# A two-layer trunk: SwiGLU blocks by seven block products in place of eight

## The chip, the cores and the metric

The kernel runs on one core of a Trainium2 chip. The metric is the device time of one execution in microseconds (us), and a run's figure is the median of its executions. The core has a matrix engine (TensorE: PE in the profile, PEld for its weight loads), VectorE (DVE), ScalarE (ACT), GpSimd (POOL) and SyncE (SP), which issues the transfers. SBUF is the memory on the core, PSUM the small one that the matrix engine writes.

## What is computed

Two layers over 512 tokens of width 1024, all float32. Each layer has a SwiGLU block, a token mixer, and a second SwiGLU block; so there are four SwiGLU blocks with an inner dimension of 2816, and two mixers (a convolution beside sparse attention; a short convolution beside stick-breaking attention).

```python
def _swiglu(x, w_in, w_out):
    gate, up = jnp.split(x @ w_in, 2, axis=-1)
    return (jax.nn.silu(gate) * up) @ w_out
...
    for layer in range(DEPTH):
        x = x + 0.5 * _swiglu(_rmsnorm(x, ffn1_norm[layer]), ffn1_w_in[layer], ffn1_w_out[layer])
        h = _rmsnorm(x, mix_norm[layer])
...
        x = x + y
        x = x + 0.5 * _swiglu(_rmsnorm(x, ffn2_norm[layer]), ffn2_w_in[layer], ffn2_w_out[layer])
    return _rmsnorm(x, final_norm)
```

## The kernel before

The stream `xT` stays in SBUF, transposed: 8 tiles of 128 channels by 512 tokens. A float32 operand is used as two parts, a high one in the matrix engine's float32r type and the rest, so one product of a weight block takes three matmuls: high by high, high by low, low by high (`mm3`, lines 112 to 115). The two parts are made by `split` (lines 80 to 87): ScalarE writes the high part (line 83), VectorE subtracts it from the source (line 84); with a scale per partition these are lines 86 and 87. `load_w` (lines 98 to 110) loads a piece of a weight of up to 128x1024 (line 103, from SP's queue) and splits it; raw pieces and split pieces have three buffers each.

`ffn` (lines 178 to 220) is a SwiGLU block. For each of 22 pairs of a gate tile and an up tile it loads the two weight pieces and runs 8 x 3 matmuls of 128x512 for each, into a PSUM bank `gu`. VectorE multiplies both by `rstd`, the reciprocal norm by token (lines 191 and 195), ScalarE applies SiLU (193), VectorE multiplies (197), and the activation is split (199). Then `down` (lines 201 to 210) makes each of the 8 output tiles `fo` with 22 x 3 matmuls, and VectorE adds half of it to `xT` (line 210). In the last block of all, the last output tile is made in two halves of 256 tokens, so that the final norm of the first half (`last`, lines 795 to 822) runs beside the second half.

After each output tile, `nxt` (for the next norm: `Norm.add`, lines 139 to 141) makes the next operand of that tile, the tile times its gain, split (`operand`, 122 to 127), and adds its square to a running sum (`square`, 129 to 137: ScalarE squares, GpSimd adds in line 136, VectorE adds the last). `finish` turns the sum into `rstd` (`rsqrt_rows`, 146 to 175: eight small matmuls, twelve small VectorE instructions, a transpose). At the start the tiles of x and the first two weight pieces are loaded in turn, so that the first product runs while x comes in (lines 751 to 762).

The order on each queue is made by the framework's scheduler, which places instructions by their priority (the order in which they are traced) and by a simulated time line; a tile's slot is given out again when its last reader is placed. GpSimd does little beside the sums of squares: in `mixer0` it scales probabilities (line 622).

Of the kernel before, what the change touches and what calls it, by code (L numbers as in the profile page):

```python
# [7 lines left out]
F32 = mybir.dt.float32  # L8
# [6 lines left out]
P = 128  # L15
# [16 lines left out]
OFFT = [0, 512, 1024, 896]  # L32
# projections beside each head
FILL = [3, 1, 1, 2, 1, 1, 2, 1]
# [11 lines left out]
def trunk(ctx: ExitStack, tc: tile.TileContext, a: dict, out: bass.AP):  # L46
# [7 lines left out]
    xnp = ctx.enter_context(tc.tile_pool(name="xnp", bufs=16))  # L54
# [25 lines left out]
    def split(hi, lo, src, scale=None):  # L80
        """hi + lo = src (times a per-partition scale), both float32r."""
# [36 lines left out]
    class Norm:  # L118
        def __init__(self, col):
            self.col, self.h, self.l, self.ss = col, [], [], []  # L120

        def operand(self, k):
            hi = xnp.tile([P, T], F32R, tag="xn", name=nm("xh"))
            lo = xnp.tile([P, T], F32R, tag="xn", name=nm("xl"))
            split(hi, lo, xT[:, k, :], prm[:, self.col + k:self.col + k + 1])
            self.h.append(hi)
            self.l.append(lo)

        def square(self, k):
            sq = cp.tile([P, T], F32, tag="c", name=nm("sq"))  # L130
            S.activation(sq, xT[:, k, :], AF.Square)  # L131
            if k == 0:
                self.ss = [sq]
            else:
                s2 = cp.tile([P, T], F32, tag="c", name=nm("ss"))
                (V if k == KD - 1 else G).tensor_tensor(s2, self.ss[0], sq, ALU.add)  # L136
                self.ss = [s2]

# [39 lines left out]
    def ffn(norm, w_in, w_out, nxt, ph, halves=None):  # L178
        act = []
        tiles = [ph.rtile("act", "act", T) for _ in range(2 * NP)]  # L180
        for p_ in range(NP):
            ps = []
            for gu in range(2):
                hi, lo = load_w(w_in[p_, :, gu], KD * P)
# [742 lines left out]
```

## Time and profile before

| | |
|---|---|
| median of 3 runs (lowest, highest) | 1989.33 us (1986.51, 1997.28) |
| span of the profiled execution | 1989.2 us |
| PE busy | 1964.9 us |
| DVE, ACT, POOL busy | 1003.6, 713.8, 107.1 us |
| read from HBM | 175.74 MB, 89 GB/s over the span |

The profiled span is within 0.2 us of the median, so sums made against the span hold for the median as well. A matmul's duration in the profile overlaps with its neighbours; its cost in a stream is the step from one start to the next.

### The profile page before, as it was taken

Reading aid. Unit: us, or ns where it says so; the run is one execution under the profiler, and the core shown is the slowest. Engines: PE = TensorE matmul, PEld = TensorE weight load, DVE = VectorE, ACT = ScalarE, POOL = GpSimd, SP = SyncE. Lnnn points to the kernel's source line nnn. Section 1 sums busy time; section 2 is a strip of 40 time slices with the busy share of each in tenths; the row PEclk is TensorE's granted clock in tenths of the full one; section 3 lists DMA queues with packets and bytes.
Section 4 is the critical chain, followed back from the end, with each engine's and each line's share of the span. In section 5 each row is a group of like instructions: output and inputs, shape, how many; then the busy total and the mean of one; then the engine's idle time right before and its main releaser. Section 6 shows DMA issues by size and latency. Waiting matters only on the chain.

```text
span 1989.2 us, 22201 instructions
## 1 busy us (share of the span) xinstructions
PE 1964.9 (99%) x8886; PEld 1598.3 (80%) x8886; DVE 1003.6 (50%) x1488; ACT 713.8 (36%) x1052; POOL 107.1 (5%) x112
## 2 busy tenths in 40 slices
PE   8999999989999999999999999999999999999998
PEld 7888888778767888888888888888877888888887
DVE  6444432499976544443334444333668744444323
ACT  5332222236675323322223333222544433322222
POOL 2000001000322100000000000000000010000000
PEclk9999999999989999999999999999999999999999
DMA  5222333232101223233332222333311222223332
GB/s 180 96 96 96 96 93 97 87 108 75 43 1 34 98 97 100 96 93 91 95 102 97 96 95 96 89 97 101 96 64 53 85 96 96 96 95 96 96 93 96
DMA packets 52086, 179.27 MB, mean 90 GB/s; under 512 B 5776, under 2 KB 6160, under 8 KB 51984
## 3 DMA queue, kind: packets, MB, share of 16 engines
q1 hardware_dynamic: 51840, 177.73, 28.0%
q8 instruction: 69, 1.13, 0.2%
q14 instruction: 33, 0.27, 0.0%
q10 hardware_dynamic: 144, 0.14, 0.0%
HBM read 175.74 MB, written 2.10 MB: 89 GB/s over the span
## 4 chain that ended last, share of the span: by engine, by line
PE 97%; DVE 1%; ACT 0%; DMA 0%; issue 0%; DVEq 0%; SPq 0%
PE gu L113 16%; PE gu L115 16%; PE gu L114 16%; PE fo L115 8%; PE fo L114 8%; PE fo L113 8%; PE ac L115 3%; PE ac L114 3%; PE ac L113 3%; PE mo L114 1%; PE mo L115 1%; PE mo L113 1%; PE pt L286 1%; PE ss L613 1%; PE po L297 1%; PE po L296 1%
## 5 line engine op out<-in xcount | busy, mean ns | idle before, releaser
L83 ACT ACTIVATE whi<-raw 128x1024 fp32r<-128x1024 f32 (+3 forms) x339 | 350.4, 1034 | 1072.5 <-PE gu L114 572.5
L84 DVE TENSOR_TENSOR wlo<-raw,whi 128x1024 fp32r<-128x1024 f32 (+3 forms) x339 | 405.7, 1197 | 302.6 <-ACT whi L83 300.0
L113 PE MATMUL gu<-xh,whi 128*128 128x512 f32 x1408 | 548.5, 390 | 6.7 <-ACT whi L83 6.7
L114 PE MATMUL gu<-xl,whi 128*128 128x512 f32 x1408 | 548.9, 390 | 0.0
L115 PE MATMUL gu<-xh,wlo 128*128 128x512 f32 x1408 | 548.5, 390 | 0.0
L113 PEld LDWEIGHTS gu<-xh,whi 128*128 128x128 f32 x1408 | 265.0, 188 | 61.5 <-ACT whi L83 6.9
L115 PEld LDWEIGHTS gu<-xh,wlo 128*128 128x128 f32 x1408 | 264.9, 188 | 55.2
L114 PEld LDWEIGHTS gu<-xl,whi 128*128 128x128 f32 x1408 | 264.9, 188 | 55.0
L115 PE MATMUL fo<-act,wlo 128*128 128x512 f32 (+1 forms) x726 | 281.9, 388 | 0.0
L113 PE MATMUL fo<-act,whi 128*128 128x512 f32 (+1 forms) x726 | 281.8, 388 | 0.0
L114 PE MATMUL fo<-act,whi 128*128 128x512 f32 (+1 forms) x726 | 281.8, 388 | 0.0
L195 DVE TENSOR_TENSOR u<-gu,rstd 128x512 f32<-128x512 f32 x88 | 60.8, 691 | 263.0 <-PE gu L115 263.0
L114 PEld LDWEIGHTS fo<-act,whi 128*128 128x128 f32 x726 | 136.3, 188 | 31.2
L115 PEld LDWEIGHTS fo<-act,wlo 128*128 128x128 f32 x726 | 136.3, 188 | 31.1
L113 PEld LDWEIGHTS fo<-act,whi 128*128 128x128 f32 x726 | 136.3, 188 | 31.0
L191 DVE TENSOR_TENSOR g<-gu,rstd 128x512 f32<-128x512 f32 x88 | 60.8, 691 | 182.7 <-PE gu L115 172.4
L113 PE MATMUL ac<-xh,whi 128*128 128x512 f32 x288 | 112.9, 392 | 0.6 <-ACT whi L83 0.6
L114 PE MATMUL ac<-xl,whi 128*128 128x512 f32 x288 | 113.1, 393 | 0.0
L115 PE MATMUL ac<-xh,wlo 128*128 128x512 f32 x288 | 113.0, 393 | 0.0
L136 POOL TENSOR_TENSOR ss<-sq,sq 128x512 f32<-128x512 f32 x7 | 11.5, 1648 | 1331.8 <-ACT sq L131 1331.8
L83 ACT ACTIVATE act<-h 128x512 fp32r<-128x512 f32 x88 | 55.8, 634 | 58.3 <-DVE h L197 58.3
L136 POOL TENSOR_TENSOR ss<-ss,sq 128x512 f32<-128x512 f32 x35 | 56.5, 1616 | 307.9 <-ACT sq L131 245.6
(277 smaller groups left out, 1854.7 us busy)
## 6 DMA issues: line engine op xcount, KB each, us to landing
raw<-in_w_in SPq DMA_DIRECT2D x174, 512.0 KB, 3.7
raw<-in_w_out SPq DMA_DIRECT2D x66, 448.0 KB, 3.3
raw<-in_w_out SPq DMA_DIRECT2D x33, 512.0 KB, 3.5
raw<-in_cd_a SPq DMA_DIRECT2D x20, 512.0 KB, 3.5
raw<-in_ab_a SPq DMA_DIRECT2D x16, 512.0 KB, 3.2
raw<-in_ab_w_out SPq DMA_DIRECT2D x8, 512.0 KB, 3.5
raw<-in_cd_w_out SPq DMA_DIRECT2D x8, 512.0 KB, 3.5
xT<-in_x SPq DMA_DIRECT2D x8, 256.0 KB, 5.5
```

The lines of the kernel that those rows point to most:

```text
L83: S.activation(hi, src, AF.Copy)
L84: V.tensor_tensor(lo, src, hi, ALU.subtract)
L113: PE.matmul(o, wh, xh, start=start, stop=False, **kw)
L114: PE.matmul(o, wh, xl, start=False, stop=False, **kw)
L115: PE.matmul(o, wl, xh, start=False, stop=stop, **kw)
L136: (V if k == KD - 1 else G).tensor_tensor(s2, self.ss[0], sq, ALU.add)
L191: V.tensor_tensor(g, ps[0], rstd, ALU.mult)
L195: V.tensor_tensor(u, ps[1], rstd, ALU.mult)
L286: PE.transpose(pt[:, w:w + P], src[:, OFFQ[i] + t * P:OFFQ[i] + (t + 1) * P], ident)
L296: PE.matmul(po[:, t * P:], vs[t], th[:, s_], start=first and t == 0, stop=False, **kw)
L297: PE.matmul(po[:64, t * P:], vs[t][:, 0], tl[:, s_], start=False, stop=last and t == NT - 1, **kw)
L613: PE.matmul(ps[:, :w], qst[h][rg, ts], klo[br][rg, :w], start=False, stop=True)
```

## The change

Each product of a SwiGLU block is cut into 2 x 2 blocks: the tokens into two halves of 256 (`TH`), the inner dimension of the product and its output dimension into two halves as well. The two-by-two block product is then made with seven block products in place of eight. Four sums of blocks are needed of the weights, four of the moving operand, and the results are combined as they accumulate.

An `up` step makes two gate tiles and two up tiles at once (11 steps in a block) from four raw weight blocks of 128x1024. A `down` step makes four output tiles from a group of 3, 3, 3 or 2 steps' activations (`CHUNKS`), twice for each group, and its weight blocks are 128x768 or 128x512. Up steps and down steps are interleaved: a group's down steps follow the up step after it, and the last two products of a step are traced behind the first product of the next.

Per step: four sums of raw weight blocks on GpSimd (`s[1]` to `s[4]`); seven splits of a block (ScalarE and VectorE), one of them with the sign turned; seven products, each of n x 2 x 3 matmuls of 128x256 (n is 4 in an up step); and after each product the `taps`. In an up step the taps are three copies out of PSUM and two SiLUs on ScalarE, eight VectorE instructions of 512 columns and one on GpSimd; then the activation's four sums on GpSimd and its split in seven parts (`Seven`). In a down step the taps are seven additions to `xT` on VectorE. A norm in front of a SwiGLU block now makes its operand by pairs of tiles (`pair`): two scaled copies on ScalarE, four sums and two splits on VectorE.

The start loads all of x before the first weights. At the end the final norm of both halves comes behind the last product. The mixers keep their work; their tiles are taken from other pools. The core of the diff:

```diff
+    def sums(e, b, t):
+        x = [b[:, i * TH:(i + 1) * TH] for i in range(4)]
+        y = [t[:, i * TH:(i + 1) * TH] for i in range(4)]
+        e.tensor_tensor(y[0], x[1], x[0], ALU.subtract)
+        e.tensor_tensor(y[1], x[3], x[0], ALU.subtract)
+        e.tensor_tensor(y[2], x[3], y[0], ALU.add)
+        e.tensor_tensor(y[3], y[2], x[2], ALU.subtract)
+    class Seven:
+        def __init__(self, hi, lo, b, t, e):
+            self.hi, self.lo = hi, lo
+            sums(e, b, t)
+            split(hi[:, :3 * TH], lo[:, :3 * TH], b[:, TH:])
+            split(hi[:, 3 * TH:], lo[:, 3 * TH:], t)
...
+        def pair(self, i):
+            b, t = (ph_[0].wide(n) for n in ("xb", "xt"))
+            v = b.rearrange("p (s t) -> p s t", t=TH)
+            for k, o in zip(PAIR[i], (v[:, 0:2][:, ::-1], v[:, 2:4])):
+                S.activation(o, xT[:, k, :].rearrange("p (s t) -> p s t", t=TH), AF.Copy, scale=self.gain(k))
+            self.ops[i] = Seven(slot("xh"), slot("xl"), b, t, V)
...
+    def seven(ph, blocks, n, ops, taps):
+        w = 2 * n * P
+        raw = {}
+        for b in ("11", "12", "22", "21"):
...
+            nc.sync.dma_start(raw[b], blocks[b])
+        s = {i: ph.tile("ws", "ws", 1024)[:, :w] for i in (1, 2, 3, 4)}
+        G.tensor_tensor(s[1], raw["21"], raw["22"], ALU.add)
+        G.tensor_tensor(s[2], s[1], raw["11"], ALU.add)
+        G.tensor_tensor(s[3], raw["11"], raw["21"], ALU.add)
+        G.tensor_tensor(s[4], s[2], raw["12"], ALU.add)
+        X, Y, W = (ph.bank(t, t) for t in ("px", "py", "pw"))
+        def product(name, o, src, op, first, sign=None):
+            hi = wsp.tile([P, 1024], F32R, tag="whi", name=nm("whi"))[:, :w]
+            lo = wsp.tile([P, 1024], F32R, tag="wlo", name=nm("wlo"))[:, :w]
+            split(hi, lo, src, sign)
+            for k in range(n):
+                for j in range(2):
+                    sl = slice((j * n + k) * P, (j * n + k + 1) * P)
+                    mm3(o[:, j * TH:(j + 1) * TH], hi[:, sl], lo[:, sl], *ops[k][op],
+                        first and k == 0 and j == 0, k == n - 1, skip_group_check=True)
+            taps(name, o)
+        product("1", X, raw["11"], S_11, True)
+        yield
+        product("2", Y, raw["12"], S_21, True)
+        product("6", X, s[2], S_T2, False, -1.0)
+        product("7", W, s[3], S_T3, True)
+        product("5", X, s[1], S_T1, False)
+        yield
+        yield lambda i: (product("3", X, s[4], S_22, False) if i == 3 else
+                         product("4", W, raw["22"], S_T4, False))
...
+        def up(s):
...
+                if m in "165":
+                    t[m] = ph.tile("c" + m)
+                    S.activation(t[m], o, AF.Copy)
+                elif m == "2":
+                    g = t["1"]
+                    V.tensor_tensor(g, o, g, ALU.add)
+                    V.tensor_tensor(halves(g), halves(g), row(0), ALU.mult)
+                    S.activation(g, g, AF.Silu)
+                elif m == "3":
+                    g = t["3"] = ph.tile("g")
+                    V.tensor_tensor(halves(g), halves(o), row(1), ALU.mult)
+                    S.activation(g, g, AF.Silu)
+                    V.tensor_tensor(v[:, 0:4:3], halves(t["5"]), halves(g), ALU.mult)
+                elif m == "4":
+                    u = t["6"]
+                    V.tensor_tensor(u, o, u, ALU.add)
+                    V.tensor_tensor(halves(u), halves(u), row(0), ALU.mult)
+                    V.tensor_tensor(v[:, 1:3], halves(u), halves(t["1"]), ALU.mult)
+                    act[s] = Seven(ph.rtile("ah", "act", 1792), ph.rtile("al", "act", 1792), blk, ph.wide("ht"), G)
+                if m == "5":
+                    u = t["5"]
+                    V.tensor_tensor(u, t["w"], u, ALU.add)
+                    G.tensor_tensor(halves(u), halves(u), row(1), ALU.mult)
...
+        def down(c0, n, q, end):
...
+            def add(r, c, o, f):
+                x = xT[:, m0 + 2 * r:m0 + 2 * r + 2, c * TH:(c + 1) * TH]
+                V.scalar_tensor_tensor(x, halves(o), f, x, op0=ALU.mult, op1=ALU.add)
...
+            if end and last and q == 1:
+                for c in range(2):
+                    last(c, m0)
+            elif end:
+                for m in (m0, m0 + 2, m0 + 1, m0 + 3):
+                    nxt(m)
...
+        prev = None
+        for i, (is_up, g) in enumerate(work):
+            flush = prev and i == len(work) - 2
+            if flush:
+                next(prev)
+            next(g)
+            if prev and not flush:
+                next(prev)
+            next(g)
+            prev = g
+        next(prev)
...
-        return Phase(dict(act=2 * NP, d=6), "b", b=7, n=1)
+        return Phase(dict(F=4, d=5, act=6, rb=3, ws=4), "F", "px", px=2, py=2, pw=2, n=1)
```

## Rows read from the trace of the kernel before

**Rows 1.** The page: busy time in us (share) xinstructions; the chain that ended last.
```profile
PE 1964.9 (99%) x8886; PEld 1598.3 (80%) x8886; DVE 1003.6 (50%) x1488; ACT 713.8 (36%) x1052; POOL 107.1 (5%) x112
...
PE 97%; DVE 1%; ACT 0%; DMA 0%; issue 0%; DVEq 0%; SPq 0%
```

**Rows 2.** Time line of PE (start us, us): first and last of three streams.
```profile
99.71 0.39 PE L113 MATMUL gu<-xh,whi 128*128 128x512 f32 x1
...
103.79 0.39 PE L113 MATMUL gu<-xh,whi 128*128 128x512 f32 x1
...
1934.77 0.39 PE L115 MATMUL fo<-act,wlo 128*128 128x512 f32 x1
...
1959.97 0.39 PE L115 MATMUL fo<-act,wlo 128*128 128x512 f32 x1
1960.20 0.28 PE L113 MATMUL fo<-act,whi 128*128 128x256 f32 x1
...
1967.92 0.28 PE L115 MATMUL fo<-act,wlo 128*128 128x256 f32 x1
```

**Rows 3.** Groups by form: line engine op out<-in xcount | busy, mean ns | idle before.
```profile
L84 DVE TENSOR_TENSOR wlo<-raw,whi 128x1024 fp32r<-128x1024 f32 x266 | 327.4, 1232 | 197.5 <-ACT whi L83 197.2
L83 ACT ACTIVATE whi<-raw 128x1024 fp32r<-128x1024 f32 x266 | 282.4, 1062 | 813.4 <-PE gu L114 544.7 <-issue 150.2 <-PE fo L114 55.5
L197 DVE TENSOR_TENSOR h<-s,u 128x512 f32<-128x512 f32 x88 | 60.9, 692 | 10.9 <-ACT s L193 1.9 <-ACT whi L83 0.5
L191 DVE TENSOR_TENSOR g<-gu,rstd 128x512 f32<-128x512 f32 x88 | 60.8, 691 | 182.7 <-PE gu L115 172.4 <-ACT rstd L175 10.2
L84 DVE TENSOR_TENSOR act<-h,act 128x512 fp32r<-128x512 f32 x88 | 60.3, 685 | 1.0 <-ACT act L83 0.7
L193 ACT ACTIVATE s<-g 128x512 f32<-128x512 f32 x88 | 55.4, 630 | 1.5 <-DVE g L191 1.4
L84 DVE TENSOR_TENSOR th<-pt,th 128x256 fp32r<-128x256 f32 x24 | 9.8, 409 | 1.6 <-ACT th L83 1.6
```

**Rows 4.** Time line of DVE and POOL at the start, 7 to 26 us.
```profile
7.40 0.69 DVE L84 TENSOR_TENSOR wlo<-raw,whi 128x512 fp32r<-128x512 f32 x1
...
11.33 1.29 POOL L136 TENSOR_TENSOR ss<-sq,sq 128x512 f32<-128x512 f32 x1 [10.89 <-ACT sq L131]
11.81 1.37 DVE L84 TENSOR_TENSOR wlo<-raw,whi 128x512 fp32r<-128x512 f32 x1 [0.81 <-ACT whi L83]
...
16.63 3.90 POOL L136 TENSOR_TENSOR ss<-ss,sq 128x512 f32<-128x512 f32 x2 [1.65 <-ACT sq L131]
16.63 7.51 POOL L136 TENSOR_TENSOR ss<-ss,sq 128x512 f32<-128x512 f32 x4 [1.65 <-ACT sq L131]
20.70 4.52 DVE L84 TENSOR_TENSOR wlo<-raw,whi 128x1024 fp32r<-128x1024 f32 x2 [1.32 <-ACT whi L83]
```

**Rows 5.** Time line of DVE and POOL in mixer0's output projection, 643 to 648 us.
```profile
643.57 4.59 DVE L87 SCALAR_TENSOR_TENSOR xl<-xT,prm,xh 128x512 fp32r<-128x512 f32 x3
644.28 3.33 POOL L136 TENSOR_TENSOR ss<-ss,sq 128x512 f32<-128x512 f32 x2
```

**Rows 6.** Time line of POOL and DVE in mixer0, 541 to 544 us (pt is in PSUM).
```profile
541.50 2.53 POOL L584 TENSOR_TENSOR lq<-lq,lq 128x512 f32<-128x512 f32 x2
542.16 1.27 DVE L84 TENSOR_TENSOR th<-pt,th 128x512 fp32r<-128x512 f32 x2
```

**Rows 7.** Time line at a block's end, 1027 to 1030 us.
```profile
1028.26 0.72 ACT L86 ACTIVATE xh<-xT,prm 128x512 fp32r<-128x512 f32 x1
1029.54 0.75 DVE L87 SCALAR_TENSOR_TENSOR xl<-xT,prm,xh 128x512 fp32r<-128x512 f32 x1
```

**Rows 8.** The first matmuls (time line), and all down matmuls of one line: first and last start.
```profile
6.71 0.80 PE L113 MATMUL gu<-xh,whi 128*128 128x512 f32 x1 [6.71 <-ACT whi L83]
11.57 0.51 PE L114 MATMUL gu<-xl,whi 128*128 128x512 f32 x1
...
L115 PE MATMUL fo<-act,wlo x726: 279/392/398, 250.4 to 1978.3; 128*128 128x512 f32 x171, 128*128 128x256 f32 x11
```

More of the change, by code (lines that the diff above doesn't have):

```diff
@@ new lines, in xtiles @@
+    def xtiles(s, n, dt=F32R):
+        ts = []
+        for i in range(n):
+            if i % 3 == 0:
+                x = slot(s, dt)
+            ts.append(x[:, (i % 3) * T:(i % 3 + 1) * T])
+        return ts
+    def sums(e, b, t):
[5 more added lines that the diff above has]
+        e.tensor_tensor(y[3], y[2], x[2], ALU.subtract)
@@ new lines, in ffn, with row, taps @@
+    def ffn(norm, w_in, w_out, nxt, ph, last=None):
+        act = {}
+        def row(c):
+            return rstd[:, c * TH:(c + 1) * TH].unsqueeze(1).to_broadcast([P, 2, TH])
+        def up(s):
+            t = {}
+            blk = ph.wide("hb")
+            v = halves(blk)
+            def taps(m, o):
+                if m in "165":
[21 more added lines that the diff above has]
+                    G.tensor_tensor(halves(u), halves(u), row(1), ALU.mult)
+                if m == "7":
+                    t["w"] = o
+            blocks = {b: w_in[s, n] for n, b in enumerate(("11", "21", "12", "22"))}
+            g = seven(ph, blocks, 4, norm.ops, taps)
+            yield next(g)
+            yield next(g)
+            f = next(g)
+            f(3)
+            f(4)
+            yield
+        def down(c0, n, q, end):
+            m0 = 4 * q
+            def add(r, c, o, f):
+                x = xT[:, m0 + 2 * r:m0 + 2 * r + 2, c * TH:(c + 1) * TH]
+                V.scalar_tensor_tensor(x, halves(o), f, x, op0=ALU.mult, op1=ALU.add)
+            def taps(m, o):
+                for r, c, f in {"1": [(0, 0, -0.5)], "2": [(0, 0, -0.5)], "6": [(1, 0, 0.5)], "7": [(1, 1, 0.5)],
+                                "5": [(1, 1, 0.5)], "4": [(1, 0, 0.5)], "3": [(0, 1, -0.5)]}[m]:
+                    add(r, c, o, f)
+            w = 2 * n * P
+            blocks = {b: w_out[q, i, :, 8 * c0 * P // 4:8 * c0 * P // 4 + w] for i, b in enumerate(("11", "21", "12", "22"))}
+            g = seven(ph, blocks, n, [act[c0 + k] for k in range(n)], taps)
+            yield next(g)
+            yield next(g)
+            f = next(g)
+            f(4)
+            f(3)
+            if end and last and q == 1:
[4 more added lines that the diff above has]
+                    nxt(m)
+            yield
+        firsts = [sum(CHUNKS[:i]) for i in range(len(CHUNKS))]
+        work, done = [], 0
+        for i, (c0, n) in enumerate(zip(firsts, CHUNKS)):
+            for s in range(done, min(c0 + n + 1, NP // 2)):
+                work.append((True, up(s)))
+            done = min(c0 + n + 1, NP // 2)
+            work += [(False, down(c0, n, q, i == len(CHUNKS) - 1)) for q in range(2)]
+        prev = None
[9 more added lines that the diff above has]
+        next(prev)
@@ L324, in taps_pe @@
             split(wh, wl, w)
-            x = [[xtile("cx") for _ in range(2)] for _ in range(2)]
+            x = xtiles("cx", 4)
+            x = [x[:2], x[2:]]
             split(*x[0], conv[j])
@@ L793, in gain, with last @@
         return prm[:, P_NF + m:P_NF + m + 1]
[L795 removed]
+    def last(c, m0):
         ts = slice(c * TH, (c + 1) * TH)
         parts = [nf.ss[0][:, ts]]
[L799 to L805 removed]
+        xg = [xT[:, m, ts] for m in range(m0)]
+        for m in range(m0, KD, 2):
+            sq = ctile("sq")
+            S.activation(halves(sq), xT[:, m:m + 2, ts], AF.Square)
+            parts += [sq[:, :TH], sq[:, TH:]]
+            x = ph.tile("xg")
+            for j in range(2):
+                xg.append(x[:, j * TH:(j + 1) * TH])
+                V.tensor_scalar(xg[-1], xT[:, m + j, ts], gain(m + j), None, op0=ALU.mult)
         rsqrt_rows(lambda s: ph.bank(s, "n"), parts, 1.0 / D, RMS_EPS, rcol[:, 2 * c:2 * c + 2], None)
```

188 lines of the change are left out of this document (81 added, 107 removed).

## The prediction

> **What bounds the kernel now.** First the page's busy times and its chain [rows 1]: the matrix engine is busy for 1964.9 of 1989.2 us and carries 97% of the chain that ended last. VectorE is at 50%, ScalarE at 36%, GpSimd at 5%. So time can only be won by fewer or shorter matmul steps, and an engine beside it has to be loaded about twice as much before it matters. Second the pace of the matmuls, from the time line [rows 2]: 18 steps of 128x512 in an up product take 4.08 us, 0.2267 us each; 108 steps in a down product take 25.20 us, 0.2333 each; 65 steps of 128x256 at the very end take 7.72 us, 0.1188 each. Half the width costs 51 to 52% of a step, so the weight load (one for each matmul, twice as often for the same columns) hides behind 256 columns as well. A SwiGLU block is 22 x 2 x 24 = 1056 up steps and 8 x 66 = 528 down steps: 239.4 + 123.2 = 362.6 us, four times 1450 of the 1989 us. Third, what the other engines' instructions cost, by form [rows 3], and what they cost when VectorE and GpSimd work at once [rows 4 to 6].
>
> **Matmuls: what is removed.** An up step has 7 products of 4 x 2 x 3 = 24 matmuls of 256 columns: 168, or 19.96 us at 0.1188. Eleven of them are 1848 matmuls. Down has 7 x n x 2 x 3 = 42n for each step, 84n for each group, n summing to 11: 924; a step of n = 3 is 14.97 us, of n = 2 9.98 us. Together 2772 x 0.1188 = 329.3 us for a block in place of 362.6. If the matrix engine went on to set the end, that would be 33.3 us for a block, 133 us in all.
>
> **VectorE beside it.** I sort its instructions by where they read, for a reason that comes next. Two inputs in SBUF: seven low parts of 128x1024, six at 1.232 us and the one with the sign at about 1.29 (1.232 and the 0.06 by which the form with a scalar, 0.75 [rows 7], exceeds 0.692 [rows 3]); the activation's two low parts, 128x768 at 0.96 (half-way between 0.685 for 512 and 1.232 for 1024) and 1.232; four taps at 0.692. That is 7.39 + 1.29 + 2.19 + 2.77 = 13.6 us for an up step. One input in PSUM: four taps at 0.691, 2.8 us. Together 16.4 us beside 19.96 us of matmuls: 82%, if nothing slows it. ScalarE: 7 x 1.062, about 1.9 for the activation's high parts, five at 0.63: 12.5 us, not a bound. A down step of n = 3 has 6 x 0.96 + 1.0 = 6.8 us with two inputs in SBUF and 7 x 0.691 = 4.8 us of additions from PSUM; of n = 2, 4.9 and 4.8 us. The weight bytes stay the same and stay hidden.
>
> **GpSimd beside it.** Four sums of 1024 columns, a product of 512 and four sums of 256 are 5632 columns for an up step, eleven times 512. Undisturbed, an addition of 512 took 1.27 to 1.29 us [rows 4, 6], so by columns 11 x 1.29 = 14.2 us. A fixed part in the 1.29 would make the long sums cheaper and the short ones dearer; I take it as even. The Trainium skill, GPSIMD Engine Reference, section 3.1, has 4497 ns for a tensor addition of 2048 columns; by that and 1.29 for 512, an estimate is 13.7 us. A down step has 3072 columns, 7.7 us (n = 3), or 2048, 5.2 us (n = 2).
>
> **The two at once.** This is the row on which I decide. From 16.63 us GpSimd adds four times 512 in 7.51 us (the first two take 3.90, so the last two run from 20.53 on), where 4 x 1.29 = 5.2 would do, and at 20.70 VectorE's two low parts of 1024 take 4.52 us in place of 2.4 [rows 4]. A low part of 512 that starts inside a GpSimd addition takes 1.37 us in place of 0.69, while the addition stays at 1.29 [rows 4]. Three of VectorE's operations take 4.59 in place of 2.1 us, beside two GpSimd additions that take 3.33 in place of 2.58 [rows 5]. With one of VectorE's inputs in PSUM nothing of this shows: 1.27 us for two, and 2.53 for GpSimd's two [rows 6]. So operations of VectorE with two SBUF inputs and GpSimd's additions take turns at something. How much both get done together, in units of their undisturbed times: from 644.28 to 647.61 VectorE 0.87 us (2.13 less 0.71 before and 0.55 after) and GpSimd 2.58, 1.04 in each us; from 11.81 to 12.62 0.13 and 0.81, 1.16; from 20.70 to 24.14 VectorE 1.30 (2.38 less 1.08 after) and GpSimd 2.46 (of 2.58 in the 3.61 us of its last two), 1.09. I take 1.08, with 1.00 and 1.16 as ends.
>
> An up step then needs (13.6 + 14.2) / 1.08 = 25.8 us for these two, against 19.96 us of matmuls. They become the bound: VectorE is busy all the time, GpSimd most of it, and the matrix engine waits for low parts. In a down step the additions from PSUM can run beside GpSimd's sums: (6.8 + 7.7 - 4.8) / 1.08 + 4.8 = 13.8 us if all do, 18.2 if none does; against 14.97 of matmuls I take 15.5. For n = 2 the ends are 9.5 and 14.1; I take 11. A block: 11 x 25.8 + 6 x 15.5 + 2 x 11 = 284 + 93 + 22 = 399 us, 36 more than before; four blocks **+145 us**. With 1.16 the up step is 24.0 and a block 374 (downs at the matmuls' 15 and 10), +45 in all.
>
> **Ends of blocks, start and tail.** (a) In the last group the last up step is finished ahead of the first down step (`flush`), which needs its activation: three taps 2.1, ScalarE 0.85 (between 0.63 and 1.06), VectorE 0.96, about 4 us to the first part; the second half of the parts waits for four GpSimd sums too (2.6) and a split (2.3), 7 us. A third of the first products does not need it. I take 5 us a block, +20 (0 to 36). (b) At a block's end four output tiles become complete together. Before it was one, and its operand (an addition of 0.69, then 0.72 and 0.75 us, [rows 7]) was covered by seven others. In front of a SwiGLU block the last two pairs now take 0.69 + 1.43 + 1.6 (four sums of 256 at 0.41, [rows 3]) + 0.96 = 4.7 us for the first and 3.8 (1.6 + 0.96 + 1.23) more for the second, with two pairs' matmuls (1.4 us for each product that can start) as cover: 5 us between the two neighbouring blocks, 3 behind each mixer, 2 in front of each mixer, whose operands need no sums: +15 (5 to 25). (c) At the start the first matmul comes at 6.71, runs slower up to about 11.6 (durations of 0.80 to 0.51 us) and then at 0.227 [rows 2, 8]: by 24 us some 65 steps, 15 us of work. Now x goes first and VectorE makes four pairs of 3.8 us, from about 7.4 on, when its first low part starts now [rows 4]: the first product ends at about 24, with 2.9 us of work. +12 (6 to 18). (d) The last matmul starts at 1978.3 [rows 8], 11 us before the end. With both halves' norms behind it, one more chain of small operations and two more scalings on each of two engines: +5 (2 to 9). Together **+52**.
>
> The mixers' own 539 us keep their work: 0. Sum: 1989.2 + 145 + 52 = 2186 us; span and median agree, so nothing is added. I forecast **2186 us**.
>
> **Rivals.** *Exclusive turns* (2290 us): the two never overlap. The Trainium skill, SBUF — State Buffer, section "SBUF: two separate sides", says that the port pair which VectorE's two-input operations and GpSimd share is an exclusive lock held for a whole instruction. The trace agrees in part: a low part inside an addition got almost nothing, but all three stretches give more than 1.00. As a mechanism here: an up step takes 27.8 us, a down step 16 and 11.5 (the additions from PSUM still run beside), a block 425, +62, four times 249, and the same 52. What speaks for it is that single sums were slowed by the rest of the instruction that was running; against it the 1.04 to 1.16.
>
> *The matrix engine still sets the end* (1908 us, faster): 1989.2 - 133 + 52. It is the case if GpSimd's sums mostly run while VectorE reads PSUM or waits, so that the two rarely meet. The block breaks even where 11 up steps take 362.6 - 13 (its share of the 52) - 110 (its down steps) = 240 us, 21.8 us each, a joint rate of 27.8 / 21.8 = 1.28. Nothing in the rows is that high, and VectorE has only 2.8 us of PSUM reading in an up step against 14.2 us of GpSimd's. For it: the rows are short stretches, and sums for a later step could slip into VectorE's pauses; but 16.4 us of 19.96 leave few.
>
> *A loose port* (2045 to 2120 us): joint rate 1.16 or a little more; then the up step nears the matmuls' time and the ends weigh about half. *Chains beside the port* (above 2330): a product waits for the tap that reads the bank it adds to, which on VectorE's queue stands behind low parts of 2.3 us. This would put the ends of all my terms together: 2330 to 2380.
>
> **How the numbers follow.** Forecast (2120 to 2240) 0.50; exclusive turns (2240 to 2330) 0.20; loose port (2040 to 2120) 0.12; chains (above 2330) 0.03; matrix engine (1880 to 1979) 0.11; between them, 0.04. The range 2040 to 2330 holds 0.82; the forecast, the loose port and the exclusive turns make its ends. A measurement of this kernel tells about 0.5% from no change, 10 us: faster 0.11, same 0.04, slower 0.85.
>
> **What would show it.** Right: in the up stretches VectorE busy for 95% or more, the 128x1024 low parts well above 1.232 us on average (about 1.7 to 2.0), GpSimd's sums of 1024 above 2.6 us, the matrix engine busy for some 75 to 80%, its pauses ended by VectorE's `wlo`; in the down stretches of three the matmuls nearly without pauses; 128x256 steps of 0.119 us where they run back to back. Wrong: low parts near 1.23 us beside busy GpSimd, or matmul steps longer than 0.119; up steps at 20 us would mean that the port does not matter; at 28 or more, that it is exclusive or that a chain of waits rules. What would upset the sum most is an up step off by 2 us: 88 us in all.

## The result, and the profile after

The changed kernel takes 2191.74 us (median of four runs, 2189.06 to 2198.77); the kernel before took 1993.16 beside it. The ratio is 1.0997, with a 95% interval of 1.0948 to 1.1045: slower by 10%. The forecast was 2186 us, from 2040 to 2330. The profiled execution spans 2191.5 us, 202.3 more than before, so the profile can stand for the median.

The page of the changed kernel, busy time first, then the slices and the chain that ended last:

```profile
PE 1940.4 (89%) x13596; PEld 1795.0 (82%) x13596; DVE 1976.3 (90%) x2092; ACT 1034.6 (47%) x1467; POOL 1195.4 (55%) x633
...
PE   4889898889999788998968998988999988998987
...
DVE  8999999889876799999998999998758769999997
...
POOL 5776766400132676777655777774100057767763
PEclk9999999999999899999978999999999989999998
...
PE 44%; DVE 34%; issue 11%; POOL 5%; ACT 3%; DMA 2%; DVEq 0%; SPq 0%; ACTq 0%; POOLq 0%
```

Against [rows 1], the matrix engine's share of the chain falls from 97% to 44%, and VectorE has 34%. Within the SwiGLU blocks the slices have VectorE at 8 and 9 and GpSimd at 5 to 7 (4 at a block's edge); in the mixers (slices 9 to 13 and 29 to 32) GpSimd is at 0 to 3.

The groups by form, VectorE's and then GpSimd's, which answer to [rows 3] and [rows 4]:

```profile
L91 DVE TENSOR_TENSOR wlo<-ws,whi 128x1024 fp32r<-128x1024 f32 x132 | 258.5, 1960 | 3.2 <-ACT whi L90 3.1
L91 DVE TENSOR_TENSOR wlo<-raw,whi 128x1024 fp32r<-128x1024 f32 x147 | 252.6, 1720 | 46.5 <-ACT whi L90 45.2 <-PE ac L121 1.4
...
L91 DVE TENSOR_TENSOR wlo<-rb,whi 128x1024 fp32r<-128x1024 f32 x44 | 108.9, 2474 | 6.2 <-ACT whi L90 6.2
...
L337 DVE SCALAR_TENSOR_TENSOR xT<-px,xT 128x512 f32<-128x512 f32 x128 | 86.9, 679 | 6.9 <-PE px L122 6.9
L313 DVE TENSOR_TENSOR c<-c,rstd 128x512 f32<-128x512 f32 x44 | 75.5, 1716 | 1.3
...
L260 POOL TENSOR_TENSOR ws<-ws,raw 128x1024 f32<-128x1024 f32 x44 | 137.0, 3114 | 90.9 <-issue 72.3 <-DVE wlo L91 18.6
...
L258 POOL TENSOR_TENSOR ws<-ws,raw 128x1024 f32<-128x1024 f32 x44 | 116.9, 2656 | 55.5 <-issue 46.4 <-POOL ws L257 8.6
```

The same subtraction of 128x1024 that took 1.232 us now takes 1.72 to 2.47 on average. The addition of 512 columns with one input in PSUM (`xT<-px`) takes 0.679, no more than such operations before (0.691 [rows 3]): only the operations with two inputs in SBUF are slowed, and the additions of GpSimd with them. What the matrix engine waits for, in the view of its waits:

```profile
PE px L122 <- DVE wlo L91: 88.6, 62, 8.7
PE px L120 <- DVE xT L337: 29.1, 22, 1.7
```

One SwiGLU block, the second, divided into stretches (busy us of each engine, number of instructions, granted clock, share and rate of the transfers). The first three rows together are its first four up steps and two down steps; the fourth and fifth together are a group of three up and two down steps, and the sixth is another; the last is its last up step, the flush and the last two down steps (with 2.3 us of the next block). The borders but the first and the last lie where a step's second product starts (`py<-xh` in an up step, `py<-ah` in a down step). A *period* is three up and two down steps, from such a start to the next, that begin behind a pair of down steps; a block has two:

```profile
724.70:762.80 38.10, 27.09 (x206) 26.34 (x205) 27.61 (x33) 17.17 (x21) 25.06 (x9) 0.82 0.35 123
762.80:833.60 70.80, 60.52 (x477) 58.64 (x476) 70.57 (x49) 32.44 (x40) 54.75 (x27) 0.98 0.23 70
833.60:871.60 38.00, 34.67 (x285) 33.84 (x284) 36.60 (x35) 15.31 (x19) 25.73 (x13) 1.00 0.36 122
871.60:938.80 67.20, 61.03 (x477) 59.81 (x476) 64.44 (x47) 31.22 (x38) 48.60 (x22) 0.95 0.24 73
938.80:974.80 36.00, 34.16 (x285) 33.71 (x284) 35.06 (x35) 15.32 (x19) 28.34 (x13) 1.00 0.37 122
974.80:1080.40 105.60, 94.52 (x759) 92.46 (x758) 102.31 (x80) 46.54 (x57) 74.90 (x36) 0.98 0.26 83
1080.40:1138.00 57.60, 43.88 (x316) 41.82 (x315) 51.83 (x55) 26.47 (x39) 31.19 (x19) 0.85 0.25 83
```

The period of rows four and five runs from the first of these matmuls to the second:

```profile
871.57 0.28 PE L120 MATMUL py<-xh,whi 128*128 128x256 f32 x1
974.77 0.28 PE L120 MATMUL py<-xh,whi 128*128 128x256 f32 x1
```

The kernel's eight periods take 103.2 to 105.6 us, 104.5 on average.

In the second row VectorE (third number in the list) is busy for 70.57 of 70.80 us: it has no time left. In the first and the last row nobody is: 27.61 of 38.10 and 51.83 of 57.60. These are the ends of the block, with waits of their own. Where the time went, from the first to the last matmul of each stretch in both traces: the four blocks took 1460.7 us and take 1645.3 (416.5, 824.0 for the two neighbouring ones, 404.9), +184.6; the mixers between them +4.6; the first matmul comes at 14.9 us in place of 6.7 [rows 8], +8.2; behind the last one there are 15.8 us in place of 10.9, +4.9. Together 202.3.

### The profile page after: what moved, and what is told of

Read it like the earlier page. It is cut to its first block, busy times and chain, and to the rows that moved or that the text cites. A ratio compares the mean times of both kernels' runs of the same rounds, so it can differ in the third digit from the quotient of the medians.

```text
span 2191.5 us, 33755 instructions
## 1 busy us (share of the span) xinstructions
PE 1940.4 (89%) x13596; PEld 1795.0 (82%) x13596; DVE 1976.3 (90%) x2092; ACT 1034.6 (47%) x1467; POOL 1195.4 (55%) x633
## 4 chain that ended last, share of the span: by engine, by line
PE 44%; DVE 34%; issue 11%; POOL 5%; ACT 3%; DMA 2%; DVEq 0%; SPq 0%; ACTq 0%; POOLq 0%
DVE wlo L91 12%; PE px L122 5%; PE px L120 5%; PE px L121 5%; DVE al L91 4%; DVE c L313 3%; DVE xT L337 3%; PE ac L121 3%; PE ac L122 3%; PE ac L120 3%; PE pw L122 3%; PE pw L120 2%; PE pw L121 2%; DVE wlo L94 2%; DMA raw<-in_w_out 2%
## 5 line engine op out<-in xcount | busy, mean ns | idle before, releaser
L122 PE MATMUL px<-xh,wlo 128*128 128x256 f32 x1408 | 419.8, 299 | 75.3 <-DVE wlo L91 72.1
L120 PE MATMUL px<-xh,whi 128*128 128x256 f32 x1408 | 416.1, 296 | 41.7 <-ACT whi L90 14.9
L121 PE MATMUL px<-xl,whi 128*128 128x256 f32 x1408 | 413.4, 294 | 7.6 <-DVE xl L91 7.6
L91 DVE TENSOR_TENSOR wlo<-ws,whi 128x1024 fp32r<-128x1024 f32 (+2 forms) x228 | 402.5, 1767 | 3.9 <-ACT whi L90 3.1
L122 PEld LDWEIGHTS px<-xh,wlo 128*128 128x128 f32 x1408 | 286.4, 204 | 86.4 <-DVE wlo L91 82.8
L120 PEld LDWEIGHTS px<-xh,whi 128*128 128x128 f32 x1408 | 286.8, 204 | 46.1 <-ACT c L299 15.9
L90 ACT ACTIVATE whi<-ws 128x1024 fp32r<-128x1024 f32 (+2 forms) x228 | 214.5, 942 | 220.6 <-PE px L121 97.3
L121 PEld LDWEIGHTS px<-xl,whi 128*128 128x128 f32 x1408 | 286.6, 204 | 8.0 <-DVE xl L91 8.0
L260 POOL TENSOR_TENSOR ws<-ws,raw 128x1024 f32<-128x1024 f32 (+2 forms) x76 | 216.8, 2852 | 119.6 <-issue 87.1
L120 PE MATMUL px<-ah,whi 128*128 128x256 f32 x704 | 205.6, 292 | 50.3 <-DVE xT L337 29.1
L258 POOL TENSOR_TENSOR ws<-ws,raw 128x1024 f32<-128x1024 f32 (+2 forms) x76 | 180.3, 2372 | 105.9 <-issue 70.3
```

The source lines that it names most:

```text
L90: S.activation(hi, src, AF.Copy)
L91: V.tensor_tensor(lo, src, hi, ALU.subtract)
L120: PE.matmul(o, wh, xh, start=start, stop=False, **kw)
L121: PE.matmul(o, wh, xl, start=False, stop=False, **kw)
L122: PE.matmul(o, wl, xh, start=False, stop=stop, **kw)
L258: G.tensor_tensor(s[2], s[1], raw["11"], ALU.add)
```

## The experiments

The theory: GpSimd's additions and VectorE's operations with two inputs in SBUF take turns; their joint work, not the matmuls, sets the pace of the up steps. Rivals: VectorE's queue by itself is too long; the matrix engine is slowed by 256-wide matmuls; chains of waits at the blocks' ends carry the loss.

### All sums on VectorE

```
-        G.tensor_tensor(s[1], raw["21"], raw["22"], ALU.add)      (and s[2] to s[4])
+        V.tensor_tensor(s[1], raw["21"], raw["22"], ALU.add)
-   act[s] = Seven(..., ph.wide("ht"), G)
+   act[s] = Seven(..., ph.wide("ht"), V)
-   G.tensor_tensor(halves(u), halves(u), row(1), ALU.mult)
+   V.tensor_tensor(halves(u), halves(u), row(1), ALU.mult)
```

> The changed kernel with every sum that stood on GpSimd (four of the weights, four of the activation, one product by the norm) moved to VectorE; the same arithmetic. Theory (the two engines take turns at something whenever VectorE has two inputs in SBUF): VectorE then holds 13.6 + 2.8 + 4.9 + 0.7 + 1.6 = 23.7 us an up step and 6.8 + 4.8 + 3.8 = 15.4 us a down step of three, 101.9 us for the repeating three up and two down steps, where the changed kernel's trace shows about 104. So although VectorE, busy 99% there, takes on 7.3 us more for each up step, the time falls a little: 2110 to 2170 us, with the 128x1024 low parts back at 1.23 us and VectorE still busy 95% or more. Rival (VectorE is full by its own work and GpSimd relieves it): the 7.3 and 3.8 us come on top, some 420 us in all, 2600 us.

Measured: 2042.58 us, ratio to before 1.0269 [1.0215, 1.0324]: 149 us less than the changed kernel, although VectorE now does everything. The page, the low parts and the time line of this kernel:

```profile
PE 1900.9 (94%) x13596; PEld 1766.1 (87%) x13596; DVE 1844.8 (91%) x2616; ACT 1030.7 (51%) x1467; POOL 105.8 (5%) x109
```

```profile
L91 DVE TENSOR_TENSOR wlo<-raw,whi 128x1024 fp32r<-128x1024 f32 x147 | 181.1, 1233 | 25.0 <-ACT whi L90 24.2 <-PE cw L122 0.4
L91 DVE TENSOR_TENSOR wlo<-ws,whi 128x1024 fp32r<-128x1024 f32 x132 | 160.1, 1214 | 3.3 <-ACT whi L90 2.4
```

```profile
799.84 1.21 DVE L91 TENSOR_TENSOR wlo<-raw,whi 128x1024 fp32r<-128x1024 f32 x1
800.97 1.21 DVE L258 TENSOR_TENSOR ws<-ws,raw 128x1024 f32<-128x1024 f32 x1
802.11 0.68 DVE L337 SCALAR_TENSOR_TENSOR xT<-pw,xT 128x512 f32<-128x512 f32 x1
802.71 1.21 DVE L259 TENSOR_TENSOR ws<-raw,rb 128x1024 f32<-128x1024 f32 x1
```

VectorE's busy time falls by 132 us while it does 524 instructions more: the low parts are back at 1.21 to 1.23 us. The direction is the theory's, the size is not: I had expected 2110 to 2170, with VectorE busy for 95% or more, and it is at 91%. The time line shows why. An operation recorded as 1.21 us is followed by the next after 1.13 or 1.14; one of 0.68 after 0.60. Back to back each costs some 0.08 us less than its row says. The 26 operations of an up step are then 23.7 - 26 x 0.08 = 21.6 us. With two down steps at their matmuls' 15.0 us (VectorE's 18 operations there come to 14.0) a period is 94.8 us, and the trace has 94.7.

### The weight sums alone on VectorE

> The changed kernel with the four sums of weights moved to VectorE; the activation's four sums and the product by the norm stay on GpSimd (4.3 us an up step, undisturbed). Taking turns: VectorE's own 21.3 us and the part of GpSimd's 4.3 us that does not fall beside its 2.8 us of reading PSUM, 24 to 25 us an up step: between the changed kernel and the one with all on VectorE, 2140 to 2190 us. Rival (GpSimd relieves VectorE): 4.9 us more an up step on a full VectorE, above 2400 us.

Only the first of the edits above, so that GpSimd keeps the activation's sums and one product, 4.2 of its 13.6 us. Measured: 2072.78 us, ratio 1.0403 [1.0372, 1.0434], GpSimd 22% busy, a period of 96.1 us (95.7 to 97.7). It lies 30 us above the kernel with all sums on VectorE and 119 below the changed one: between, as both the amount of GpSimd's reading and the time go, but under the 2140 to 2190 expected, which was worked out without the 0.08 us as well.

### No weight sums

```
-        s = {i: ph.tile("ws", "ws", 1024)[:, :w] for i in (1, 2, 3, 4)}
-        G.tensor_tensor(s[1], raw["21"], raw["22"], ALU.add)      (and s[2] to s[4])
+        s = {1: raw["22"], 2: raw["11"], 3: raw["21"], 4: raw["12"]}
```

> The changed kernel without the four sums of weights: the products 6, 7, 5 and 3 take raw blocks in their place (that part of the computation is left out); the buffers of the sums go to the raw blocks. Theory: GpSimd has 4.3 us an up step left, VectorE 16.4 and some waiting, 19 to 20 us, about the matmuls' 19.96; the matrix engine sets the end again: 1905 to 1970 us, its steps at 0.119 us, low parts at 1.23 to 1.4 us. Rival (the time went to the narrow matmuls, to the longer chains between product, tap and product, or to the ends of blocks): these all stay, and so do 2100 us or more.

Measured: 1964.39 us (one run, span 1962.6), inside the 1905 to 1970. The page, and the two matmuls between which one of its periods runs:

```profile
PE 1880.3 (96%) x13596; PEld 1758.9 (90%) x13596; DVE 1554.2 (79%) x2092; ACT 1033.5 (53%) x1467; POOL 340.4 (17%) x329
```

```profile
142.35 0.28 PE L120 MATMUL py<-xh,whi 128*128 128x256 f32 x1
232.66 0.28 PE L120 MATMUL py<-xh,whi 128*128 128x256 f32 x1
```

The matrix engine is 96% busy, and a period takes 90.3 us, where its matmuls alone (3 x 168 + 2 x 126 of them at 0.1195) are 90.3. So the matrix engine sets the pace once the weight sums are gone, and the 256-wide steps are not slow by themselves. This is about the floor of this blocking as it stands, 28 us under the kernel before (1992.16 beside it). The predicted 133 us of matmuls are nearly there in the periods, but the four blocks take 1408.6 us from their first to their last matmul, where all their matmuls at 0.1195 would be 1325: some 83 us go at the blocks' ends, and the start, the first mixer and the tail are 25 us longer than before.

### The same sums as fills

```
-        G.tensor_tensor(s[1], raw["21"], raw["22"], ALU.add)      (and s[2] to s[4])
+        for i in (1, 2, 3, 4):
+            G.memset(s[i], 0.5)
```

> The changed kernel with GpSimd's four weight sums replaced by four fills of the same tiles with a constant: GpSimd writes as many columns to the same places but reads nothing from SBUF, and VectorE, ScalarE and the matrix engine do all that they did. Left out: the four weight sums. If it is GpSimd's reading that VectorE's two-input operations take turns with, the low parts of 128x1024 fall from 1.7 to 1.96 us back to 1.23 to 1.3 and the time comes near that of the run without the sums (1964 us): 1950 to 1990, a little more where fills last long and delay a product. If writing is enough, the low parts stay above 1.5 us and the time stays above 2060.

Measured: 1962.55 us (one run, span 1960.7), as fast as without the sums. The forms and, around 763 us, the time line of both engines:

```profile
L91 DVE TENSOR_TENSOR wlo<-ws,whi 128x1024 fp32r<-128x1024 f32 x132 | 168.3, 1276 | 22.8 <-ACT whi L90 22.8
```

```profile
L258 POOL MEMSET ws<- 128x1024 f32 x176 | 167.4, 954 | 445.9 <-DVE wlo L91 291.4 <-DVE wlo L94 145.9 <-DVE xl L91 6.4
```

```profile
763.22 0.74 POOL L258 MEMSET ws<- 128x768 f32 x1
...
763.20 0.94 DVE L91 TENSOR_TENSOR wlo<-raw,whi 128x768 fp32r<-128x768 f32 x1
```

A fill of GpSimd and a low part of VectorE run through the same 0.7 us, both at their undisturbed times. In the whole trace 17 low parts of 1024 columns meet a fill and nothing else of GpSimd's, and take 1.214 us on average, 1.219 at most; 78 meet one of the operations that GpSimd still has to do (the activation's sums, the product by the norm, the squares) and take 1.60, and these keep the mean of the form shown at 1.276. GpSimd writing to SBUF costs VectorE nothing; its reading does. The whole gain in time is not that alone: a fill is also shorter than an addition (0.95 us in place of 2.35) and waits for no load, which shows at the blocks' starts (below).

### A third of the matmuls left out

```
-   mm3(o_j, hi, lo, xh, xl, ...)
+   PE.matmul(o_j, lo, xh, ...)
+   PE.matmul(o_j, hi, xl, ...)
```

> The changed kernel with two matmuls in place of three for each block of the SwiGLU products (high by high left out); all else stays. The matrix engine's time for an up step falls from 19.96 to 13.3 us, by 110 us a block, 440 us in all. Theory (VectorE and GpSimd set the pace of the up steps): little of it is seen, 2110 to 2185 us; what is seen comes from the down steps, the ends of blocks and the start. Rival (the matrix engine sets the pace with its pauses behind narrow matmuls): some 300 us or more, 1890 or less.

Measured: 2155.55 us (one run), a period of 102.3 us in place of 104.5. With a third of the SwiGLU matmuls gone, some 440 us of the matrix engine's time, the kernel gains 36. Some of the 440 us comes back, as the granted clock falls from 0.956 to 0.896 on average: some 1290 steps are spaced 0.21 us and not 0.12, 120 us in all, 60 more than in the changed kernel. That leaves 380 us of which 36 are seen: the matrix engine is not what sets the pace of the changed kernel.

### GpSimd's additions beside the kernel before

```
+        if extra:                                  (set during the SwiGLU blocks)
+            G.tensor_tensor(junk[:, :n], raw[:, :n], raw[:, :n], ALU.add)
```

> The kernel before, with one GpSimd addition more for each weight piece of its four SwiGLU blocks: as wide as the piece (1024, or 1024 and 384 columns), it adds the raw piece to itself and writes into a tile that nothing reads. VectorE is half idle there. My theory, that what counts is the pair's joint time against the matmuls' time: the low parts that meet an addition are slowed (mean of the 128x1024 ones 1.6 to 2.4 us in place of 1.23), yet VectorE's and GpSimd's work for one piece (1.23 + 2.35, over 1.08, 3.3 us, and the taps) stays under the 5.4 us of its 24 matmuls, so the time stays within 0.5% of before: 1983 to 2003. Rival, that GpSimd's work costs wherever it meets VectorE, because a slowed low part delays the product that waits for it: 132 pieces for a block, 1 us each on average for half of them, 4 x 66 = 264 us, or at any rate over 2030.

Not shown in these two lines are the tile `junk` and a smaller scratch for transfers from GpSimd's queue, of which this kernel issues none. Measured: 1992.16 us beside 1989.97, ratio 1.0011 [0.9985, 1.0037]: no change that can be told. GpSimd's busy time goes from 5% to 34%:

```profile
L84 DVE TENSOR_TENSOR wlo<-raw,whi 128x1024 fp32r<-128x1024 f32 x266 | 378.0, 1422 | 142.4 <-ACT whi L83 142.1
L84 DVE TENSOR_TENSOR wlo<-raw,whi 128x896 fp32r<-128x896 f32 x66 | 100.7, 1525 | 95.9 <-ACT whi L83 93.6
```

The low parts are slower (1.42 us on average, less than the 1.6 expected: 83 of the 266 of 1024 columns meet an addition and take 1.87, the others 1.22), and nothing follows from it, because VectorE had half its time free [rows 1]. So in this pair of kernels contention costs where the two engines' joint work exceeds the matmuls beside it, and not where it stays under them.

### The last group not waiting for its last activation

```
-   g = seven(ph, blocks, n, [act[c0 + k] for k in range(n)], taps)
+   g = seven(ph, blocks, n, [act[min(c0 + k, 9)] for k in range(n)], taps)
```

> The changed kernel, whose last group of down steps multiplies by the activation before the last in place of the last one, which is still computed. It leaves out the last 256 inner rows' share of the output. This takes away the wait of the flush alone: the pair of last down steps no longer waits for the taps, the sums and the splits of the last up step. In the prediction the flush was 5 us a block: 2172 us (2165 to 2180). Read from the trace of the changed kernel, the first of the two last down steps loses 11 to 14 us in each block: 2135 to 2155. If VectorE's queue is what runs behind there and not the wait for this one activation, the time stays at 2185 to 2195.

Measured: 2172.45 us, 19.3 us under the changed kernel, 4.8 a block (the runs of the two kernels spread over 10 and 3 us). The prediction's 5 us for the flush stands; the 11 to 14 us that I had read from the idle time there were not all the flush.

### Sums made by transfers

Two of the four weight sums can be had from the transfers: a plain load of one block into the sum's tile and an accumulating transfer of the other, from GpSimd's queue. All other sums are on VectorE, as in the first experiment.

```
+   for i, b, c in ((1, "21", "22"), (3, "11", "21")):
+       nc.sync.dma_start(s[i], blocks[b])
+       G.dma_start(s[i], blocks[c], accum_op=ALU.add)
```

> The kernel with all sums on VectorE (e1_all_on_vector, 2042.6 us), with two of its four weight sums made by the transfers instead: 21 is loaded once more into the tile of the sum and 22 added to it by an accumulating transfer from GpSimd's queue, and 11 and 21 likewise. GpSimd's engine still reads nothing from SBUF. VectorE loses two operations of 1.15 us in an up step: 21.6 - 2.3 = 19.3 us, under the 19.96 us of the matmuls, so the matrix engine should set the pace again: a period of three up and two down steps at 90.3 to 91.5 us in place of 94.8, with the last steps some 16 us a block, 4 x 16 = 64: 1980 us (1960 to 1995), at or a little under the kernel before. Rival: the transfers are now the limit. They move twice the bytes (8 pieces of 512 KB for an up step, 4.2 MB in 20 us or 210 GB/s, and the profile of the changed kernel shows no slice over 134 GB/s), and a sum that comes late holds its product: over 2045.

Measured: 2136.45 us, ratio 1.0717 [1.0687, 1.0746], 94 us slower than the kernel it was to improve. VectorE's waits and the rate in 40 slices:

```profile
DVE ws L260 <- DMA ws<-in_w_in: 133.6, 28, 8.5
```

```profile
GB/s 237 187 183 178 198 159 166 106 97 93 40 1 64 170 170 218 158 197 158 159 180 170 188 185 186 171 173 110 109 69 50 89 173 179 192 165 199 157 168 81
```

The hoped pace is not there: from product 2 to product 2, up steps that follow an up step take 21.5 us on average (17.3 to 26.5), and the first behind a pair of down steps 23.4 (19.7 to 25.9), where it was 15.8 with all sums on VectorE; a period is 105.2 us. VectorE waits for sums that have not landed. The rival's sign came true, its reason only in part: the transfers did reach 237 GB/s in one slice, so the 210 GB/s are not above what they can give. That a sum's load has to wait until its tile is free, and so comes late, is a guess that the next runs don't settle.

```
+   nc.sync.dma_start(s[4], blocks["12"])
+   G.dma_start(s[4], s[2], accum_op=ALU.add)
```

> As e8_two_sums_by_dma, and the fourth sum too: 12 is loaded once more and the second sum, which VectorE makes, is added to it by an accumulating transfer from SBUF to SBUF. VectorE has 18.1 us for an up step. If the pace was already set by the matmuls, the time is that of e8 within 10 us; if VectorE's queue still cost something there, 10 to 25 us less. Rival: 10 pieces for an up step, 5.2 MB in 20 us or 260 GB/s, are more than the transfers give: slower than e8 by 20 us or more.

Measured: 2351.42 us, ratio 1.1803 [1.1773, 1.1834]. With the third sum VectorE's waits for such sums rise from 133.6 to 246.5 us and the time by 215 us: slower, as this run's rival had it; whether for its reason is not shown.

Then only in the up steps (`if n == 4`), with the plain loads on GpSimd's queue as well, for two sums and for one:

> As e8_two_sums_by_dma (2136 us), but in the up steps alone, and with the plain loads of the two sums on GpSimd's queue too, so that no load of a raw piece stands behind one that waits for the tile of a sum; the down steps add on VectorE again. If e8 lost its time to that queue and to the down steps' transfers, the up steps now come at 20.0 to 20.5 us and the two down steps of three at 30 to 31, a period of 90 to 92 us: 1975 to 2005. If the accumulating transfers themselves are too slow for four pieces more in 20 us, it stays over 2060.

> As e10_two_by_dma_up_only with one sum (11 and 21) by transfers and the other three on VectorE: 20.45 us of VectorE in an up step, 0.5 above the matmuls, and two pieces more for the transfers instead of four. A period of 91 to 93 us: 1985 to 2015, within 10 us above e10 if that one's transfers keep up, and under it if they don't. If one accumulating transfer for an up step already holds the products, over 2043.

Measured: 2085.87 us (ratio 1.0454 [1.0408, 1.05]) with two, 2017.59 (1.0133 [1.007, 1.0195]) with one. One sum by transfer is the best form found of this change, 174 us under it and 25 us under all sums on VectorE, with a period of 93.0 us; it is 3 us above the range expected of it and still 1.3% slower than the kernel before. With two, the period is 99.2 us where 90 to 92 were hoped for, and VectorE still waits 152.3 us for the first sum to land, with the loads off the raw pieces' queue; what sets the pace of these transfers stays open. Of the versions that compute the whole result none beats the kernel before.

## Why the forecast held

**The matmuls.** Right: 128x256 steps stand at 0.1195 us where they run back to back, 0.1188 in the prediction.

**The port.** The prediction took what VectorE's two-input operations and GpSimd's additions get done together to be 1.08 times their undisturbed work. Over a period of three up and two down steps its own prices are 3 x (13.6 + 14.2) + 2 x (6.8 + 7.7) = 112.4 us; the period lasts 104.5: 1.08. Up steps that follow an up step take 24.5 us on average (24 of them, from product 2 to product 2) where the sum said 25.8: the eight that come soonest behind a pair of down steps take 22.7 to 23.2, the other sixteen 24.2 to 27.7, 25.3 on average.

What the 1.08 stood for is another thing than I thought. It is not that the two engines share. With what operations occupy back to back (0.08 us less for each of VectorE's 13, so 12.6), and GpSimd's additions at the 2.35 us for 1024 columns and 0.73 for 256 that it shows alone (13.6 in place of 14.2), an up step is 26.2 us of work, a down step of three 13.5, a period 105.6, and the trace has 104.5. So the sum comes out to 1% with the two excluding each other for whole instructions, and only the fixed parts overlapping. A rate of 1.08 on the higher prices gives the same period, so the sum alone does not decide; the time line of the changed kernel does. GpSimd first, then VectorE:

```profile
254.89 2.61 POOL L260 TENSOR_TENSOR ws<-ws,raw 128x768 f32<-128x768 f32 x1
258.45 2.39 POOL L257 TENSOR_TENSOR ws<-rb,rb 128x1024 f32<-128x1024 f32 x1 [0.95 <-DVE wlo L94]
...
254.85 0.94 DVE L91 TENSOR_TENSOR wlo<-raw,whi 128x768 fp32r<-128x768 f32 x1
256.00 0.69 DVE L337 SCALAR_TENSOR_TENSOR xT<-pw,xT 128x512 f32<-128x512 f32 x1 [0.20 <-PE pw L122]
...
258.94 2.72 DVE L91 TENSOR_TENSOR wlo<-ws,whi 128x768 fp32r<-128x768 f32 x1
```

At 254.85 the low part of 768 is first, takes its 0.94, and the addition, which would need about 1.8 (half-way between 1.29 for 512 and 2.35 for 1024), takes 2.61. The addition from PSUM at 256.00 runs inside it in its 0.69. At 258.45 the addition is first, takes its 2.39, and the low part ends 0.82 us after it. In both pairs whoever comes second waits for the other's whole instruction. So the rival *exclusive turns* had the mechanism and wrong prices (each operation about 0.08 us too dear, which made its period 115 us and its time 2290), and the forecast had a wrong picture of the mechanism and a rate, taken from rows in the same inflated prices, that cancelled this: by that, its 25.8 us for an up step was luck in part. The Trainium skill, SBUF — State Buffer, section "SBUF: two separate sides", says that an operation of VectorE with two inputs in SBUF contends with a GpSimd instruction that reads SBUF, and not with one that only writes it. The fills agree, with 1.214 us for a low part of 1024 beside them.

**GpSimd's prices.** Sums of 1024 columns are cheaper and those of 256 dearer than by columns (2.35 and 0.73 us in place of 2.58 and 0.645). The prediction named this fixed part and left it out; it is 0.6 us of an up step. The prediction's estimate from the figure in the Trainium skill, GPSIMD Engine Reference, section 3.1, was 13.7 us for an up step; the trace agrees with 13.6.

**The down steps.** Too dear: 15.5 us, just over the 14.97 of their matmuls, as if what the port does there ended with the step. GpSimd's and VectorE's work for the next up step runs on in them, so a whole period goes by the port's sum. (One of the two ends for n = 2 should be 9.7 and not 9.5; nothing hangs on it.) Of 108.4 us that the prediction gave a period, 104.4 were used (103.2 and 105.6 in the block above): 8 us a block too much.

**The ends.** By the stretches of the second block, four up and two down steps took 146.9 us where the prediction's prices give 4 x 25.8 + 31 = 134.2: +12.7, and it had 3 for the operands behind a mixer. The last up step and the last two down steps took 57.6 less 2.3, 55.3, where 25.8 + 22 = 47.8 was priced: +7.5, and it had 5 for the flush, which by its own experiment is 4.8. What the prediction had left out is at the start of a block, on the time line of the changed kernel, by queue and engine:

```profile
715.24 0.33 SPq L255 DMA_DIRECT2D raw<-in_w_in  x1
730.84 1.28 SPq L255 DMA_DIRECT2D rb<-in_w_in  x3
...
735.75 2.35 POOL L257 TENSOR_TENSOR ws<-rb,rb 128x1024 f32<-128x1024 f32 x1 [12.80 <-DMA rb<-in_w_in]
738.17 2.34 POOL L258 TENSOR_TENSOR ws<-ws,raw 128x1024 f32<-128x1024 f32 x1
...
740.54 1.06 ACT L93 ACTIVATE whi<-ws 128x1024 fp32r<-128x1024 f32 x1 [3.71 <-POOL ws L258]
...
741.63 2.28 DVE L94 SCALAR_TENSOR_TENSOR wlo<-ws,whi 128x1024 fp32r<-128x1024 f32 x1 [6.02 <-ACT whi L93]
...
731.25 0.28 PE L122 MATMUL py<-xh,wlo 128*128 128x256 f32 x1
...
741.65 0.58 PE L120 MATMUL px<-xh,whi 128*128 128x256 f32 x1 [7.40 <-ACT whi L93]
```

SyncE's queue holds the loads of the blocks 21 and 22 back for 15.2 us, until the last operand's low part (`xl`) is done at 730.76; its waits name that operation as releaser:

```profile
SPq L255 <- DVE xl L91: 15.2, 1, 15.2
```

The loads land 4.9 us later, two dependent additions of GpSimd follow, then the high part, and the third product starts 10 us after the second has ended; its matmuls with the low part have to wait until that is done at 743.91. In the steady state the sums of a step are made while the step before multiplies; at a block's start nothing covers them. The fills, which wait for no load, show about what this costs, the port included: from product 2 of the first up step to that of the second it is 33.4, 35.9 and 36.6 us at the starts behind the beginning and the two mixers, and 25.7, 24.2 and 27.3 with fills. That the tiles of these blocks lie where the mixer's last operands lay would explain the wait for `xl`; no run moved them. Between the two neighbouring blocks the loss has another form: there these two products are 45.4 us apart, and the operands' low parts stand at 3.15 and 2.30 us beside GpSimd's additions. Most of it stays without these: 37.3 us with fills and 34.7 without weight sums.

**Start and tail.** +8.2 us for the first matmul where 12 were forecast for a late first product, +4.9 for the tail where 5 were.

So the total came within 6 us of the median because errors of both signs met, and that closeness is luck: it had some 30 us too much for the down steps of the four blocks, 10 too much because it put the blocks before at 1450 us where they took 1460.7, and 4 too much for the start; it had some 45 too little for the blocks' ends and 5 too little for the mixers, which it put at nothing. The sign and the cause didn't hang on that: with fills in place of GpSimd's weight sums the time is 1963 us, so 229 of the 2192 us are there because of these sums. The eight periods are 114 of that (104.5 us against 90.3 for each), and some 37 are in the four starts, where the wait for loads and sums comes in besides the port.

**The signs named.** VectorE over 95% in the up stretches: 70.57 of 70.80. Low parts at 1.7 to 2.0 us: 1.72 and 1.96, but 2.47 for those of the last loaded blocks. GpSimd's sums above 2.6: 2.66 to 3.11. The matrix engine at 75 to 80% there: 477 steps of 0.1195 are 57.0 of 70.80, 81%. Pauses ended by `wlo`: the longest row of the waits, 88.6 us. Down stretches nearly without pauses: not quite, 285 steps are 34.1 of 38.0 us.

## What to carry to other kernels

Before work is moved to GpSimd to relieve VectorE, sort both engines' operations by whether they read SBUF, and how often; two-input operations of VectorE and additions of GpSimd add up as on one engine, and here VectorE alone did both faster (2043 us against 2192). Price a run of short operations by the spacing of their starts, not by their recorded durations. And where a product takes operands that another engine has to prepare, count one whole uncovered preparation for each place where the pipeline begins anew.

## What the runs showed of the hardware that was not expected

Operations of VectorE that follow each other overlap by about 0.08 us, in the rows of the first experiment. GpSimd's fills of 128x1024 take 0.954 us against 2.35 for an addition, and the low parts beside them were not slowed. And pauses of the matrix engine cost it speed as well: in two stretches of the changed kernel, one in the first up steps and one in the last down steps of the first block, its matmul steps were 0.21 us for a time, and the granted clock was 0.66 on average:

```profile
30.00:40.00 10.00, 6.01 (x33) 5.81 (x34) 9.12 (x9) 3.34 (x5) 3.84 (x3) 0.66 0.41 152
400.00:410.00 10.00, 5.64 (x28) 5.13 (x27) 7.53 (x9) 3.33 (x5) 4.36 (x4) 0.66 0.08 31
```

That is the lower of its two levels, 1.2 GHz, for part of each stretch; the engine had paused just before, for 5.7 us until a low part was done in the first and for 3.6 us until an operand was in the second. Some 640 steps of the SwiGLU blocks were spaced so, 60 us more than at 0.12; how much of it reached the end of the kernel, where mostly VectorE was waited for, was not separated.
